# Layer 0 of a two-layer trunk: the turn of block 1, the order of the first products, and where weight rows 3 and 5 are split

## The chip, the cores and the metric

The kernel runs on one core of a Trainium2 chip. The metric is the device time of one execution in microseconds. The engines are TensorE (PE, with its weight loads PEld), VectorE (DVE), ScalarE (ACT), GpSimd (POOL) and the sync engine (SP), which only issues DMAs; ACT and POOL issue DMAs too.

## The reference

Two layers on x (512 tokens, 1024 channels, float32). Layer 0 mixes by causal pooling over windows of 2, 4, 8 and 16, layer 1 by differential attention; a dense SwiGLU of width 2816 follows in both.

```python
for i in range(DEPTH):                        # DEPTH = 2
    h = _multiscale_pool(x, ...) if i % 2 == 0 else _diff_attention(x, ...)
    x = _layernorm(ALPHA * x + h, ln_mix_g[i], ln_mix_b[i])
    x = _layernorm(ALPHA * x + _swiglu(x, w_gate[i], w_up[i], w_down[i]), ln_ffn_g[i], ln_ffn_b[i])

def _layernorm(x, g, b):
    return (x - mean) * lax.rsqrt(var + LN_EPS) * g + b

def _swiglu(x, w_gate, w_up, w_down):
    return (jax.nn.silu(x @ w_gate) * (x @ w_up)) @ w_down
```

The change lies where layer 0's mixer ends and its SwiGLU begins: the first normalization, the transposition of its result, and the first products with `w_gate` and `w_up`.

## The kernel before

**Split numbers.** A float32 matrix product is done as three products of rounded parts. Every operand is split into a high part (ScalarE casts it to the matmul's type, `split`, L123) and a low part (what is left, a subtraction, L124, on VectorE unless `low` names another engine). `mm3` (L147) issues high weights by high x, high weights by low x, low weights by high x.

**Rows of weights.** All weights lie in `in_wall` as rows of 128x1024. `fetch` (L107) loads a row with SP's queue into one of five `raw` buffers; a load waits until the buffer's last row is split, and all later loads of SP wait behind it. `ready(upto, low)` (L126) fetches five rows ahead and splits each row up to `upto`. Rows 0 and 1 are the pooling mixer's, rows 2 to 5 (w2 to w5) are the gate and up weights of the first two column blocks, 6 and 7 (g_4, g_5) of the third.

**The engines' order is the order of the code.** `manual_schedule` (L303) keeps each engine's instructions in program order, so an instruction that waits holds all behind it on its engine.

**The end of the mixer (L447 to L514).** The 512 tokens are four blocks of 128. For each block s: `mixed` multiplies the pooled values by the mixing weights into two banks of the accumulation memory, `summed` adds them to the residual `res` (L183) and takes statistics (L190), `spread_of` makes mean and variance (L196, L198) and GpSimd raises the variance to the power -1/2 (L199), `norm` applies both in place on VectorE (L208). `transposed` turns the block on TensorE into two banks of four 128x128 pieces (`pt`, L235). `turned` (block 0) applies gain and bias on ScalarE and splits the result into `xt`. Before `norm` of block 0, `split_pooled` casts the last pooled banks on ScalarE (L123) and subtracts on VectorE (L124).

**The turn of block 1 (`turned_apart`, L259).** For each bank, and in it for each piece, ScalarE applies gain and bias straight into the high part (L269), and VectorE the same in full precision into `y` (L272). When both banks are done, VectorE subtracts the high parts from `y` (L278). Both engines read the same bank, and one instruction waits for the other there.

**The first products (`ffn`, L821 to L845).** For the first three column blocks f the gate bank (`g`) and the up bank (`u`) are multiplied with the first 256 tokens (`lo` = 0, six products of 24 matmuls), then with the last 256 (`lo` = 256). The very first product is taken apart by banks of the turn (L649 to L658): for pieces 0 to 3 high by high, low by high, high by low, then the same for pieces 4 to 7. All others go piece by piece with `mm3`. `late` puts the turns of block 2 behind the product (1, 0) and of block 3 behind (1, 1). Behind the products come the gate (`gated`, L671), the residual's gain and bias with `gb` (L227, L228), sums of weights for the later Strassen stages (`load_terms`, L738, on GpSimd's queue), and, from the ninth column block on, Strassen products. All of these are the same in both kernels.

Of the kernel before, what the change touches and what calls it, by code (L numbers as in the profile page):

```python
# [23 lines left out]
KB = D // P  # L24
# [30 lines left out]
def trunk(ctx, tc, x, wall, pscale, lam_p, subln, table, lng, lnb, band, first, onehot, out):  # L55
    nc = tc.nc

    keep = ctx.enter_context(tc.tile_pool(name="keep", bufs=1))
# [7 lines left out]
    xt = keep.tile([P, 2, 2, KB, 256], F32R, name="xt")  # L66
# [40 lines left out]
    def fetch(upto):  # L107
        while fetched[0] < min(upto, total):
            c = fetched[0]
            raws[c] = keep.tile([P, 1024], F32, tag="raw", name=f"raw{c}", bufs=RAWS)  # L110
            nc.sync.dma_start(out=raws[c], in_=wall[rows_of_wall[c]])
            if c in added:
                nc.gpsimd.dma_start(out=raws[c], in_=wall[added[c]], accum_op=ALU.add)
            fetched[0] += 1

    def split(dst_h, dst_l, src, scale=1.0, low=None):
        if scale != 1.0:
            nc.scalar.mul(dst_h, src, scale)
            nc.vector.scalar_tensor_tensor(
                dst_l, src, scale, dst_h.bitcast(F32), op0=ALU.mult, op1=ALU.subtract  # L120
            )
        else:
            nc.scalar.copy(dst_h, src)  # L123
            (low or nc.vector).tensor_tensor(dst_l, src, dst_h.bitcast(F32), op=ALU.subtract)  # L124

    def ready(upto, low=None):  # L126
        while divided[0] < min(upto, total):
            c = divided[0]
            fetch(c + RAWS)
            h, l = weight_pair(f"w{c}")  # L130
            raw = raws.pop(c)
            if c in by_dma:
                nc.scalar.copy(h, raw)
                nc.scalar.mul(l, raw, -1.0)
                nc.gpsimd.dma_start(
                    out=l, in_=wall[rows_of_wall[c]].bitcast(F32R), accum_op=ALU.add
                )
# [92 lines left out]
    turns = {}  # L230
# [27 lines left out]

    def turned_apart(n, s):  # L259
        o = (s % 2) * P  # L260
        banks = turns.pop((n, s))
        ys = []
        for i, pt in enumerate(banks):
            y = keep.tile([P, 4, P], F32, tag="y", name=f"y{n}_{s}_{i}", bufs=2)
            for k in range(4):
                kk = 4 * i + k
                bias, scale = bT[:, n, kk : kk + 1], gT[:, n, kk : kk + 1]
                a = pt[:, k * P : (k + 1) * P]
                nc.scalar.activation(  # L269
                    xt[:, s // 2, 0, kk, o : o + P], a, AF.Identity, bias=bias, scale=scale  # L270
                )
                nc.vector.tensor_scalar(  # L272
                    y[:, k, :], a, scalar1=scale, scalar2=bias, op0=ALU.mult, op1=ALU.add
                )
            ys.append(y)
        for i, y in enumerate(ys):
            h, l = (xt[:, s // 2, j, 4 * i : 4 * i + 4, o : o + P] for j in range(2))
            nc.vector.tensor_tensor(l, y, h.bitcast(F32), op=ALU.subtract)  # L278

    def turn(n, s):  # L280
        transposed(n, s)
# [22 lines left out]
    with tc.tile_pool(name="pool", bufs=1) as pp:  # L304
# [166 lines left out]
        mixed(2, 0)  # L471
        summed(0, 1)
        spread_of(0, 0)
        ready(4, nc.gpsimd)
        split_pooled(1, 2, 3)
        norm(0, 0)
        tbh = pp.tile([33, HEADS], F32R, name="tbh")
# [18 lines left out]
        mixed(3, 1)  # L496
        turned(0, 0)
        turned_apart(0, 1)
        ready(5)
        stat(0, 2, 0)  # L500
        summed(2, 1)
        spread_of(0, 2)
        ready(6)
        norm(0, 2)
        summed(3, 0, 1)
        spread_of(0, 3)
# [19 lines left out]
    def ffn(layer, late):  # L526
        n = 2 * layer + 1
# [4 lines left out]
        with tc.tile_pool(name=f"ffn{layer}", bufs=1) as fp:  # L532
# [111 lines left out]
                if upto > len(chunks):  # L644
                    prepare(upto - len(chunks), upto - len(chunks))

            def product(acc, j, lo, hi, apart=False):
                h, l = halves[j]
                if apart:  # L649
                    for b in range(2):  # L650
                        for w, i in ((h, 0), (l, 0), (h, 1)):
                            for k in range(4 * b, 4 * b + 4):
                                nc.tensor.matmul(
                                    wide(acc, lo, hi), w[:, k * P : (k + 1) * P],
                                    x_at(k, lo, hi)[i], start=w is h and i == k == 0,
                                    stop=(i, k) == (1, KB - 1),
                                )
                    return  # L658
                for k in range(KB):
                    mm3(  # L660
                        wide(acc, lo, hi),
                        (h[:, k * P : (k + 1) * P], l[:, k * P : (k + 1) * P]),
                        x_at(k, lo, hi),
                        k == 0,
                        k == KB - 1,
                    )
# [12 lines left out]
            def sums_of_x():  # L679

                r0, r1, r2, r3 = spare(4), spare(15), spare(6), spare(17)

                def whole(t, a, b):
                    tt(t, quarter(a, 0, b).bitcast(F32), quarter(a, 1, b).bitcast(F32), op=ALU.add)

                def high(m, t):
                    nc.scalar.copy(xs[:, m, 0], t)  # L687

                def low(m, t):
                    tt(xs[:, m, 1], t, xs[:, m, 0].bitcast(F32), op=ALU.subtract)  # L690
# [24 lines left out]
                yield  # L715
# [106 lines left out]
            accs = [(bank(f"g{layer}_{f}"), bank(f"u{layer}_{f}")) for f in range(early)]  # L822
            load_terms(0)
            load_terms(1)
            sums = sums_of_x()
            for lo in (0, 256):
                for f in range(early):
                    for i in range(2):
                        product(
                            accs[f][i], 2 * f + i, lo, lo + 256, layer == f == i == lo == 0  # L830
                        )
                        if not lo and (f, i) in late:
                            late[f, i]()
# [95 lines left out]
            f = early  # L929
# [40 lines left out]
            banks = {}  # L970
            done = store if final else None
            for p in DOWN:
# [586 lines left out]
```

## Time and profile before

| | us |
|---|---|
| median of three runs | 953.36 (953.12 to 954.56) |
| the profiled execution | 953.28 |
| its span, first to last instruction | 951.5 |
| TensorE busy in the span | 931.8 (98%) |
| VectorE / ScalarE / GpSimd busy | 790.1 / 514.0 / 128.4 |

In the timelines a row is: start, duration, engine, line, operation, output<-inputs, shapes, count, and in brackets the idle time before it with what ended it. Starts count from the span's start. A matmul's row is longer than its pitch, since matmuls overlap; the difference of two starts is the time that one takes of TensorE.

### The profile page before, as it was taken

To read this page: it belongs to the slowest core of one execution; us is meant where nothing else is said; L and a number is where in the kernel's file an instruction comes from. 1 tells how busy PE (TensorE), PEld (TensorE's weight loads), DVE (VectorE), ACT (ScalarE), POOL (GpSimd) and SP (SyncE) were. 2 spreads that over 40 slices of the span, in tenths; PEclk is the share of its full clock that TensorE was granted. 3 is DMA by queue.
4 is the path that set the end of the run, shared out by engine and by line. 5 is a ranking of instruction groups with operands and counts; after the bars stand their busy time and mean duration, and the time that the engine had idled before them with its cause. 6 is when DMAs were issued, how large, how long until landed. Compare 5 with 4: busy or idle time off the path is not lost.

```text
span 951.5 us, 14946 instructions
## 1 busy us (share of the span) xinstructions
PE 931.8 (98%) x5712; PEld 830.7 (87%) x5712; DVE 790.1 (83%) x1165; ACT 514.0 (54%) x817; POOL 128.4 (13%) x153
## 2 busy tenths in 40 slices
PE   9799999999999999999999999999999999999996
PEld 8698899999988878887888878998899999988885
DVE  7859979999988579968887785779779999987778
ACT  6563245555554357766877862833344554564450
POOL 4121211110001201100211100211111110001101
PEclk9999999999999999999999999999999999999999
DMA  8477897885867996876576522396978886878942
GB/s 232 148 227 246 303 277 248 260 262 187 273 206 258 358 297 225 216 191 163 136 158 151 131 102 89 102 319 207 292 242 249 252 270 202 260 248 277 365 156 90
DMA packets 86038, 211.11 MB, mean 222 GB/s; under 512 B 15140, under 2 KB 26660, under 8 KB 85966
## 3 DMA queue, kind: packets, MB, share of 16 engines
q1 hardware_dynamic: 43420, 117.16, 37.2%
q0 software_dynamic: 18768, 58.20, 24.6%
q10 hardware_dynamic: 23778, 34.78, 10.2%
q8 instruction: 45, 0.74, 0.3%
q14 instruction: 27, 0.22, 0.1%
HBM read 173.40 MB, written 36.72 MB: 221 GB/s over the span
## 4 chain that ended last, share of the span: by engine, by line
PE 78%; DVE 9%; DMA 6%; ACT 3%; issue 2%; SPq 1%; POOL 0%; DVEq 0%; ACTq 0%; POOLq 0%
PE A L895 17%; PE C L895 8%; PE P L962 6%; PE B L895 4%; PE Q L962 3%; PE u L151 3%; PE u L150 3%; PE u L149 3%; PE g L151 3%; PE g L150 3%; PE g L149 3%; DMA r<-tsum 2%; PE va L1110 2%; PE s L1176 2%; DMA r<-in_wall 2%
## 5 line engine op out<-in xcount | busy, mean ns | idle before, releaser
L629 DVE TENSOR_TENSOR raw<-raw,raw 128x1024 f32<-128x1024 f32 x56 | 68.3, 1219 | 0.5
L123 ACT CAST xs<-hid 128x512 fp32r<-128x512 f32 (+1 forms) x60 | 34.7, 582 | 24.4 <-DVE hid L807 24.4
L124 DVE TENSOR_TENSOR xs<-hid,xs 128x512 fp32r<-128x512 f32 (+1 forms) x60 | 38.4, 642 | 7.8 <-ACT xs L123 7.8
L1192 ACT ACTIVATE p<-p,mn 128x128 f32<-128x128 f32 (+3 forms) x64 | 35.2, 552 | 12.4 <-DVE mn L1187 12.4
L249 ACT ACTIVATE y<-pt,bT,gT 128x128 f32<-128x128 f32 x72 | 27.1, 456 | 22.4 <-PE pt L235 22.3
L738 POOL DMA_DIRECT2D b<-in_wall x20 | 14.1, 708 | 171.4 <-DVE g_58l L635 66.4
L799 POOL DMA_DIRECT2D xs<-ssum x24 | 17.5, 727 | 140.2 <-PE Q L962 119.0
L671 DVE TENSOR_TENSOR hid<-sg,u 128x512 f32<-128x512 f32 x16 | 11.0, 686 | 27.7 <-PE u L151 16.9
L199 POOL TENSOR_TENSOR rs<-rs,mhalf 128x1 f32<-128x1 f32 x16 | 12.0, 751 | 155.4 <-DVE rs L198 111.8
L738 POOL DMA_DIRECT2D hid<-in_wall x24 | 18.8, 825 | 85.3 <-DMA tsum<-hid 39.5
L1187 DVE CUSTOM_DVE_ANT_0 p<-s,bias 128x128 f32<-128x128 f32 (+3 forms) x64 | 28.0, 485 | 0.7 <-PE s L1176 0.7
L775 ACT CAST v<-u 128x512 fp32r<-128x512 f32 x22 | 13.7, 622 | 27.2 <-DVE u L773 27.0
L190 DVE BATCH_NORM_STATS2 st<-res 128x6 f32<-128x512 f32 x32 | 22.2, 694 | 1.1
L921 ACT ACTIVATE sg<-sg 128x512 f32<-128x512 f32 x14 | 8.9, 634 | 26.0 <-DVE sg L914 26.0
L739 POOL DMA_DIRECT2D hid<-in_wall x12 | 14.8, 1234 | 50.1 <-DMA hid<-in_wall 50.1
L687 ACT CAST xs<-hid 128x1024 fp32r<-128x1024 f32 x8 | 8.4, 1052 | 23.9 <-DVE hid L704 11.6
L1176 PE MATMUL s<-heads 64*128 64x256 f32 (+2 forms) x168 | 20.0, 354 | 1.1 <-ACT heads L123 0.8
L124 DVE TENSOR_TENSOR xt<-y,xt 128x512 fp32r<-128x512 f32 x18 | 12.2, 689 | 8.9 <-ACT xt L123 8.9
L1176 PEld LDWEIGHTS s<-heads 64*128 64x128 f32 x168 | 14.1, 185 | 5.2 <-ACT heads L123 1.0
L910 DVE TENSOR_TENSOR hid<-C,hid 128x512 f32<-128x512 f32 x14 | 9.7, 691 | 10.8 <-PE C L895 9.3
L1206 DVE SCALAR_TENSOR_TENSOR p<-p,sm,p 128x128 f32<-128x128 f32 (+3 forms) x32 | 17.7, 552 | 1.1
L906 ACT COPY hid<-C 128x512 f32<-128x512 f32 x14 | 8.2, 588 | 18.3 <-PE C L895 18.3
(1194 smaller groups left out, 3672.4 us busy)
## 6 DMA issues: line engine op xcount, KB each, us to landing
raw<-in_wall SPq DMA_DIRECT2D x122, 512.0 KB, 4.9
r<-tsum SPq DMA_DIRECT2D x40, 512.0 KB, 4.4
hid<-in_wall POOLq DMA_DIRECT2D x36, 512.0 KB, 7.0
b<-in_wall POOLq DMA_DIRECT2D x30, 512.0 KB, 5.9
r<-in_wall SPq DMA_DIRECT2D x30, 512.0 KB, 5.1
tsum<-hid ACTq DMA_DIRECT2D x24, 512.0 KB, 5.5
ssum<-v ACTq DMA_DIRECT2D x22, 512.0 KB, 4.0
tsum<-b ACTq DMA_DIRECT2D x20, 512.0 KB, 5.0
```

The source lines that it names most:

```text
L123: nc.scalar.copy(dst_h, src)
L124: (low or nc.vector).tensor_tensor(dst_l, src, dst_h.bitcast(F32), op=ALU.subtract)
L149: nc.tensor.matmul(acc, ah, bh, start=start, stop=False)
L150: nc.tensor.matmul(acc, ah, bl, start=False, stop=False)
L151: nc.tensor.matmul(acc, al, bh, start=False, stop=stop)
L629: tt(t, raws[pair[0]], raws[pair[1]], op=ALU.add)
L738: nc.gpsimd.dma_start(out=t[:, j], in_=src[:, j])
L895: nc.tensor.matmul(o, w[:, c], x[:, kk, :], start=p in ("P1", "Q5", "P2") and f + kk + e == 0, stop=p in ("Q4", "Q3", "P2") and (f, kk, e) ...
L962: nc.tensor.matmul(accs[s], x[:, k, r], y[:, c], start=first and k == 0 and e == 0, stop=last and k == m - 1 and e == 2, skip_group_check= ...
L1176: nc.tensor.matmul(accs[c][:, :wide], a[r, qs], b[r, :wide], start=i == 0, stop=i == 2)
L1187: nc.vector.tensor_tensor_reduce(out=p, in0=accs[c][:, :w], in1=biases[h][:, w - 1 :: -1] if w < S else biases[h][:, ::-1], op0=ALU.add, o ...
L1192: nc.scalar.activation(p, p, AF.Exp, bias=mn[:, q, c : c + 1], scale=-1.0, accum_out=sm[:, q, c : c + 1],)
```

## The change

Three edits, all before the second half of the first products.

1. `turned_apart`: ScalarE makes the high part of bank 0 while VectorE makes the full values of bank 1. Then ScalarE copies bank 1's high part from VectorE's result, VectorE makes bank 0's full values, and subtracts bank 1 first, then bank 0.
2. The six products of the first 256 tokens are ordered by parts. The first (`by_half`): high by high and low by high for pieces 0 to 3, the same for pieces 4 to 7, then high by low for 4 to 7 and for 0 to 3. The five others (`by_part`): all high by high, all high by low, all low by high.
3. Row 3 is split behind the turn of block 1 instead of ahead of the last `split_pooled`, and its low part moves from GpSimd to VectorE; row 4 takes row 5's old place on VectorE, and row 5's low part moves to GpSimd.

```diff
@@ turned_apart @@
-        for i, pt in enumerate(banks):
-            y = keep.tile([P, 4, P], F32, tag="y", name=f"y{n}_{s}_{i}", bufs=2)
+        ys = [
+            keep.tile([P, 4, P], F32, tag="y", name=f"y{n}_{s}_{i}", bufs=2) for i in range(2)
+        ]
+        hs, ls = (
+            [xt[:, s // 2, j, 4 * i : 4 * i + 4, o : o + P] for i in range(2)] for j in range(2)
+        )
...
+        def in_full(i):
             for k in range(4):
-                nc.scalar.activation(
-                    xt[:, s // 2, 0, kk, o : o + P], a, AF.Identity, bias=bias, scale=scale
+                a, bias, scale = affine_of(i, k)
+                nc.vector.tensor_scalar(
+                    ys[i][:, k, :], a, scalar1=scale, scalar2=bias, op0=ALU.mult, op1=ALU.add
                 )
-                nc.vector.tensor_scalar(
-                    y[:, k, :], a, scalar1=scale, scalar2=bias, op0=ALU.mult, op1=ALU.add
-                )
-            ys.append(y)
-        for i, y in enumerate(ys):
-            h, l = (xt[:, s // 2, j, 4 * i : 4 * i + 4, o : o + P] for j in range(2))
-            nc.vector.tensor_tensor(l, y, h.bitcast(F32), op=ALU.subtract)
+
+        for k in range(4):
+            a, bias, scale = affine_of(0, k)
+            nc.scalar.activation(hs[0][:, k, :], a, AF.Identity, bias=bias, scale=scale)
+        in_full(1)
+        nc.scalar.copy(hs[1], ys[1])
+        in_full(0)
+        for i in (1, 0):
+            nc.vector.tensor_tensor(ls[i], ys[i], hs[i].bitcast(F32), op=ALU.subtract)
@@ the end of the mixer @@
         spread_of(0, 0)
-        ready(4, nc.gpsimd)
         split_pooled(1, 2, 3)
...
         turned_apart(0, 1)
-        ready(5)
+        ready(4)
         stat(0, 2, 0)
         summed(2, 1)
         spread_of(0, 2)
-        ready(6)
+        ready(5)
+        ready(6, nc.gpsimd)
         norm(0, 2)
@@ product @@
                 if apart:
-                    for b in range(2):
-                        for w, i in ((h, 0), (l, 0), (h, 1)):
-                            for k in range(4 * b, 4 * b + 4):
+                    for i, (w, e, ks) in enumerate(apart):
+                        for k in ks:
...
@@ ffn @@
+            ks = [range(4 * b, 4 * b + 4) for b in range(2)]
+            by_part = [(0, 0, range(KB)), (0, 1, range(KB)), (1, 0, range(KB))]
+            by_half = [(0, 0, ks[0]), (1, 0, ks[0]), (0, 0, ks[1]), (1, 0, ks[1])]
+            by_half += [(0, 1, ks[1]), (0, 1, ks[0])]
...
-                            accs[f][i], 2 * f + i, lo, lo + 256, layer == f == i == lo == 0
+                            accs[f][i], 2 * f + i, lo, lo + 256,
+                            None if layer or lo else by_part if f or i else by_half,
```

How the rows move on the engines. ScalarE, from the last pooled banks of the mixer (`pool_2`, `pool_3`) to the splits behind the turn of block 1 (`pt_0_*` and `y_0_*` belong to block 0, `pt_1_*` and `y_1_*` to block 1; w3h is row 3's high part). Before:

```order
L123 COPY w3h<-raw_325 128x1024
L123 COPY pooled<-pool_2_201 128x2x256
L123 COPY pooled<-pool_3_202 128x2x256
...
L269 ACTIVATE xt<-pt_1_0_436,bT,gT 128x128 x4
L269 ACTIVATE xt<-pt_1_1_437,bT,gT 128x128 x4
L123 COPY w4h<-raw_327 128x1024
L123 COPY w5h<-raw_329 128x1024
```

and with the change:

```order
L123 COPY pooled<-pool_2_201 128x2x256
L123 COPY pooled<-pool_3_202 128x2x256
...
L282 ACTIVATE xt<-pt_1_0_430,bT,gT 128x128 x4
L284 COPY xt<-y_1_1_467 128x4x128
L123 COPY w3h<-raw_325 128x1024
L123 COPY w4h<-raw_327 128x1024
L123 COPY w5h<-raw_329 128x1024
```

The cast of row 3 went from ahead of the pooled casts to behind the turn, and four of the turn's eight instructions became one copy.

GpSimd, from the power of block 0 (`rs_0`) to the first loads of weight terms into `hid`. Before:

```order
L199 TENSOR_TENSOR rs_0_362<-rs_0_362,mhalf 128x1
L124 TENSOR_TENSOR w3l<-raw_325,w3h 128x1024
L482 MEMSET line 8x128
L199 TENSOR_TENSOR rs_1_431<-rs_1_431,mhalf 128x1
L199 TENSOR_TENSOR rs_2_504<-rs_2_504,mhalf 128x1
L199 TENSOR_TENSOR rs_3_521<-rs_3_521,mhalf 128x1
L738 DMA hid_535<-in_wall 128x2x512 x2
```

and with the change:

```order
L199 TENSOR_TENSOR rs_0_362<-rs_0_362,mhalf 128x1
L490 MEMSET line 8x128
L199 TENSOR_TENSOR rs_1_425<-rs_1_425,mhalf 128x1
L199 TENSOR_TENSOR rs_2_495<-rs_2_495,mhalf 128x1
L124 TENSOR_TENSOR w5l<-raw_329,w5h 128x1024
L199 TENSOR_TENSOR rs_3_518<-rs_3_518,mhalf 128x1
L746 DMA hid_532<-in_wall 128x2x512 x2
```

The low part of row 3 left the place behind block 0's power, and that of row 5 came between the powers of blocks 2 and 3, ahead of the loads.

VectorE, from the turn of block 1 to the norm of block 2. Before:

```order
L272 TENSOR_SCALAR y_1_0_472<-pt_1_0_436,gT,bT 128x128 x4
L272 TENSOR_SCALAR y_1_1_481<-pt_1_1_437,gT,bT 128x128 x4
L278 TENSOR_TENSOR xt<-y_1_0_472,xt 128x4x128
L278 TENSOR_TENSOR xt<-y_1_1_481,xt 128x4x128
L124 TENSOR_TENSOR w4l<-raw_327,w4h 128x1024
...
L124 TENSOR_TENSOR w5l<-raw_329,w5h 128x1024
L208 TENSOR_SCALAR res<-res,mv_2_502,rs_2_504 128x1024
```

and with the change:

```order
L276 TENSOR_SCALAR y_1_1_467<-pt_1_1_431,gT,bT 128x128 x4
L276 TENSOR_SCALAR y_1_0_466<-pt_1_0_430,gT,bT 128x128 x4
L287 TENSOR_TENSOR xt<-y_1_1_467,xt 128x4x128
L287 TENSOR_TENSOR xt<-y_1_0_466,xt 128x4x128
L124 TENSOR_TENSOR w3l<-raw_325,w3h 128x1024
...
L124 TENSOR_TENSOR w4l<-raw_327,w4h 128x1024
L208 TENSOR_SCALAR res<-res,mv_2_493,rs_2_495 128x1024
```

The two banks changed places, and each split behind them is that of one row earlier.

More of the change, by code (lines that the diff above doesn't have):

```diff
@@ L260, in turned_apart, with affine_of @@
         o = (s % 2) * P
-        banks = turns.pop((n, s))
-        ys = []
-        for i, pt in enumerate(banks):
-            y = keep.tile([P, 4, P], F32, tag="y", name=f"y{n}_{s}_{i}", bufs=2)
-            for k in range(4):
[L266 to L269, printed above, removed]
-                    xt[:, s // 2, 0, kk, o : o + P], a, AF.Identity, bias=bias, scale=scale
-                )
-                nc.vector.tensor_scalar(
-                    y[:, k, :], a, scalar1=scale, scalar2=bias, op0=ALU.mult, op1=ALU.add
-                )
-            ys.append(y)
-        for i, y in enumerate(ys):
-            h, l = (xt[:, s // 2, j, 4 * i : 4 * i + 4, o : o + P] for j in range(2))
-            nc.vector.tensor_tensor(l, y, h.bitcast(F32), op=ALU.subtract)
+        pts = turns.pop((n, s))
+        ys = [
[4 more added lines that the diff above has]
+        )
+        def affine_of(i, k):
+            kk = 4 * i + k
+            return pts[i][:, k * P : (k + 1) * P], bT[:, n, kk : kk + 1], gT[:, n, kk : kk + 1]
+        def in_full(i):
+            for k in range(4):
+                a, bias, scale = affine_of(i, k)
+                nc.vector.tensor_scalar(
+                    ys[i][:, k, :], a, scalar1=scale, scalar2=bias, op0=ALU.mult, op1=ALU.add
+                )
+        for k in range(4):
[6 more added lines that the diff above has]
+            nc.vector.tensor_tensor(ls[i], ys[i], hs[i].bitcast(F32), op=ALU.subtract)
     def turn(n, s):
@@ L645, in ahead, with product @@
                     prepare(upto - len(chunks), upto - len(chunks))
-            def product(acc, j, lo, hi, apart=False):
+            def product(acc, j, lo, hi, apart=None):
                 h, l = halves[j]
                 if apart:
-                    for b in range(2):
-                        for w, i in ((h, 0), (l, 0), (h, 1)):
-                            for k in range(4 * b, 4 * b + 4):
[L653 to L657, printed above, removed]
+                    for i, (w, e, ks) in enumerate(apart):
+                        for k in ks:
+                            nc.tensor.matmul(
+                                wide(acc, lo, hi), (h, l)[w][:, k * P : (k + 1) * P],
+                                x_at(k, lo, hi)[e], start=i == 0 and k == ks[0],
+                                stop=i == len(apart) - 1 and k == ks[-1],
+                            )
                     return
```

## The prediction

> **What bounds the kernel now.** I read the page first, then the busy time by stretches, then the timeline of each engine up to 60 us, because the change touches nothing later. Two lines of the page:
>
> ```profile
> span 951.5 us, 14946 instructions
> PE 931.8 (98%) x5712; PEld 830.7 (87%) x5712; DVE 790.1 (83%) x1165; ACT 514.0 (54%) x817; POOL 128.4 (13%) x153
> ```
>
> TensorE sets the time. By stretches (busy TensorE, the granted clock, share and rate of the DMA engines):
>
> ```profile
> 39.00:42.30 3.30, 3.15 (x14) 0.50 0.07 11
> 43.00:300.00 257.00, 257.00 (x1820) 1.00 0.80 250
> ```
>
> From 43 us on TensorE has work without a break for 257 us, so whatever the start loses or saves goes to the end, as long as the weights keep up. The start does lose: in the first of these rows it runs at half the clock, and a wait of 3.35 us lies before it. TensorE's timeline at that place (start, duration, operation, in brackets the idle time and its releaser):
>
> ```profile
> 33.28 0.40 PE L653 MATMUL g<-xt,w2h 128*128 128x256 f32 x2
> 39.15 2.08 PE L653 MATMUL g<-xt,w2h 128*128 128x256 f32 x8 [3.35 <-DVE xt L278]
> 42.59 0.28 PE L149 MATMUL u<-xt,w3h 128*128 128x256 f32 x1
> 48.34 1.04 PE L235 MATMUL pt<-ident,res 128*128 128x128 f32 x8
> 49.13 0.36 PE L149 MATMUL u<-xt,w5h 128*128 128x256 f32 x1
> 52.08 1.04 PE L235 MATMUL pt<-ident,res 128*128 128x128 f32 x8
> 58.58 0.28 PE L151 MATMUL u<-xt,g_5l 128*128 128x256 f32 x1
> 58.70 0.28 PE L149 MATMUL g<-xt,w2h 128*128 128x256 f32 x1
> ```
>
> The first product runs from 33.28 to 42.59, 9.31 us. The last two rows show the pitch, 0.12 us, so its 24 matmuls are worth 2.88. The goal line is 58.70, where the second half of the columns begins: six products and two turns must lie before it, and I work out when the changed kernel gets there.
>
> **Term 1, weight row 3 leaves ScalarE's queue: 1.74 us gained.** The order before and after has this place ahead of the turn; its rows in the trace:
>
> ```profile
> 18.48 0.28 PE L411 MATMUL pool<-bh,xt 128*128 128x256 f32 x1
> 21.93 1.05 ACT L123 CAST w3h<-raw 128x1024 fp32r<-128x1024 f32 x1 [3.49 <-DMA raw<-in_wall]
> 22.89 1.07 ACT L123 CAST pooled<-pool 128x512 fp32r<-128x512 f32 x2
> 22.26 0.15 DVE L198 TENSOR_SCALAR rs<-mv 128x1 f32<-128x1 f32 x1
> 23.50 1.29 DVE L124 TENSOR_TENSOR pooled<-pool,pooled 128x512 fp32r<-128x512 f32 x2 [1.09 <-ACT pooled L123]
> 24.70 1.46 DVE L208 TENSOR_SCALAR res<-res,mv,rs 128x1024 f32<-128x1024 f32 x1
> 44.77 0.81 DVE L208 TENSOR_SCALAR res<-res,mv,rs 128x1024 f32<-128x1024 f32 x1 [0.44 <-POOL rs L199]
> 22.56 0.55 POOL L199 TENSOR_TENSOR rs<-rs,mhalf 128x1 f32<-128x1 f32 x1 [2.11 <-DVE rs L198]
> 23.09 2.41 POOL L124 TENSOR_TENSOR w3l<-raw,w3h 128x1024 fp32r<-128x1024 f32 x1
> ```
>
> ScalarE stood 3.49 us behind the transfer of row 3 while the pool banks behind it had been ready since about 18.8. Without it the two casts run at once, and VectorE's 1.09 us of idle time goes. The second piece is the 1.46 us of L208 at 24.70 against 0.81 at 44.77: it overlaps GpSimd's w3l, which ends at 25.50, and L208 ends 0.66 after that, at 26.16. Read so, it was held until GpSimd was done; with w3l gone from here 0.65 more go. Together 1.74: block 1's transposes move from 30.94 to 29.2, the first product from 33.28 to 31.54.
>
> **Term 2, the turn and the order of the product: 5.86 us gained.**
>
> ```profile
> 29.05 1.50 ACT L249 ACTIVATE y<-pt,bT,gT 128x128 f32<-128x128 f32 x4
> 30.58 0.62 ACT L123 CAST xt<-y 128x512 fp32r<-128x512 f32 x1
> 32.10 0.41 DVE L272 TENSOR_SCALAR y<-pt,gT,bT 128x128 f32<-128x128 f32 x1
> 32.55 0.46 ACT L269 ACTIVATE xt<-pt,bT,gT 128x128 fp32r<-128x128 f32 x1 [0.48 <-DVE y L272]
> 34.92 0.76 DVE L272 TENSOR_SCALAR y<-pt,gT,bT 128x128 f32<-128x128 f32 x2 [0.53 <-ACT xt L269]
> 38.41 1.28 DVE L278 TENSOR_TENSOR xt<-y,xt 128x512 fp32r<-128x512 f32 x2
> 39.61 1.22 DVE L124 TENSOR_TENSOR w4l<-raw,w4h 128x1024 fp32r<-128x1024 f32 x1
> ```
>
> Before, the two engines take turns on one bank, 0.94 us a piece (31.61 to 32.55). Apart, four pieces take ScalarE 1.5 us and VectorE 1.46 (pitch 0.35 from the pair of 0.76, plus 0.41). All new operations have such rows, so their cost is not open. After, in steps: ScalarE's bank 0 from 29.87 to 31.4; VectorE's bank 1 from 30.3 to 31.76; the copy 31.82 to 32.44; VectorE's bank 0 to 33.15; both subtractions (1.28) to 34.4. TensorE has its first eight matmuls ready at 31.54, the next eight follow to 33.46, then it waits to 33.9 and once more 0.1 for the low parts and is through at 35.0: 3.45 instead of 9.31. The cold stretch goes with the long wait. Row 3's cast now comes behind the copy (32.4 to 33.4), its low part on VectorE at 34.3 to 35.5; high weights go first, so w3l is needed 1.92 into its product, at 36.9, and covered by 1.4 us. w4l (below) ends at 39.0 and is needed at 39.8.
>
> **Term 3, what comes back: 2.8 us lost.** VectorE's sequence behind the turn is the same, moved by 39.61 - 34.3 = 5.3; TensorE is 7.6 early at 35.0. The other edit is here: row 5's low part goes to GpSimd, between two powers.
>
> ```profile
> 16.98 3.46 POOL L124 TENSOR_TENSOR w2l<-raw,w2h 128x1024 fp32r<-128x1024 f32 x1 [0.62 <-ACT w2h L123]
> 43.32 1.41 POOL L199 TENSOR_TENSOR rs<-rs,mhalf 128x1 f32<-128x1 f32 x1 [13.38 <-DVE rs L198]
> 43.10 1.23 DVE L124 TENSOR_TENSOR w5l<-raw,w5h 128x1024 fp32r<-128x1024 f32 x1
> 45.50 0.68 DVE L183 SCALAR_TENSOR_TENSOR res<-res,mix 128x512 f32<-128x512 f32 x1
> 49.38 0.81 DVE L208 TENSOR_SCALAR res<-res,mv,rs 128x1024 f32<-128x1024 f32 x1 [0.73 <-POOL rs L199]
> ```
>
> The power of block 2 took 1.41 us, to 44.73, 0.40 behind the end of VectorE's split; the same happens with w4l in w5l's place, so it ends at 39.4. Then GpSimd goes on with w5l at once, and VectorE's L208 of block 2 wants to start in the same moment. No row shows this race. The two ends: L208 runs freely (0.81, to 40.25), or it is held as at 24.70, until w5l's end plus 0.66. I take the second, since GpSimd needs no signal for its next instruction (w3l at 23.09 follows a power that ends at 23.11). At 2.41 for w5l, L208 ends at 42.5; at the 3.46 of w2l, at 43.5, which I keep as the bad end.
>
> TensorE has finished three products at 35.0 + 2 x 2.88 = 40.75 and waits to 42.6 for block 2's transposes (1.85). They take 0.8 (48.34 to 49.13), row 5's product ends at 46.3; w5l, ready at 41.8, is in time. VectorE needs 3.88 from L183 to the next L208 (45.50 to 49.38), so block 3 is normed at 47.1 and TensorE waits to 47.25 (0.95). With 0.86 for the transposes and 5.76 for two products it reaches the second half at 53.9 instead of 58.70. Block 3's ScalarE work, twice 1.50 + 0.62 from about 47.9, and the last subtraction (0.64) end near 52.8, so nothing waits there. Sum: 1.74 + 5.86 - 2.8 = **4.8 us**.
>
> The Trainium skill (SBUF — State Buffer, Who interferes with whom) speaks against the placing of w5l: a VectorE instruction in a two-port mode and a GpSimd one that reads SBUF shut each other out completely, and the one issued first wins. By that rule and the order taken here the sum is the same 4.8, with VectorE first it is that of the first rival; the 0.66 behind w3l's end agrees with it.
>
> **The queues.** SP's loads stay in order, but row 8's buffer is now freed at 35.5 instead of 25.50, and row 9's load and the two gb loads behind it wait for w5l (41.8; before, 40.86). GpSimd's first term loads come behind the later power, about 46.5 instead of 49.57. Who needs them:
>
> ```profile
> 41.23 0.43 SPq L177 DMA_DIRECT2D gb<-in_lng  x1
> 49.57 1.60 POOL L738 DMA_DIRECT2D hid<-in_wall  x2 [0.23 <-PE pt L235]
> 64.72 0.69 DVE L671 TENSOR_TENSOR hid<-sg,u 128x512 f32<-128x512 f32 x1 [6.60 <-PE u L151]
> ```
>
> VectorE first reads gb after the gate at 64.72, which becomes 59.9. That is 17 us behind its load, so I price these moves at nothing.
>
> **The rivals.** *VectorE gets in first* (20%): L208 runs its 0.81, w5l is held instead and still ends by 42.7. Block 2 costs no wait, block 3 about 0.6, the goal line moves to 51.6, a gain of 7.1: 946.2. For it speaks that the start order on the two engines differs by hundredths; against, w3l's row.
>
> *Weights don't keep up* (9%). In the first down projection the lead is small (first row: busy us of PE, PEld, DVE, ACT and POOL, the clock, the DMA engines' share and rate):
>
> ```profile
> 310.00:350.00 40.00, 39.54 (x175) 32.41 (x174) 24.09 (x27) 18.49 (x23) 8.23 (x10) 1.00 0.99 331
> L962 PE MATMUL P<-d_30l,xs x4: 388/394/397, 346.6 to 349.4; 128*128 128x512 f32 x4
> L124 DVE TENSOR_TENSOR d_30l<-r,d_30h x1: 1226/1226/1226, 344.1 to 344.1; 128x1024 fp32r<-128x1024 f32 x1
> ```
>
> The DMA engines are 99% busy and d_30l is ready 1.3 us ahead of its use (346.6 - 345.3). If that stretch stayed where it is, only 1.3 us would be left: 952.0. Against it: its loads are issued as TensorE and VectorE free their buffers, so it starts earlier too.
>
> *The clock halves again* (10%): TensorE waits 1.85 and 0.95 us. One stretch like 39.00 to 42.30 costs half of 3.3, so 950.1. Against it: the wait before 26.31 did nothing (1.00 below, TensorE busy 0.12 of 1.9 us).
>
> ```profile
> 24.40:26.30 1.90, 0.12 (x2) 0.02 (x1) 1.90 (x4) 0.17 (x1) 1.22 (x2) 1.00 0.95 390
> ```
>
> The Trainium skill (TensorE: Matmul & The Clock Gate, The HAM clock gate) lets the clock fall after a whole idle window of about 3.4 us, which neither wait fills; by it this rival would be worth nothing.
>
> *Slower* (6%): the same mechanism on all the new gaps (33.5, 40.75, 46.3), so that the clock stays at a half. It costs half of the time spent so; beyond 9.6 us of it the gain of 4.8 is gone, and through five products (14.4 us at full pitch) it costs 14.4: 962.9. The gaps would have to be taken for idleness though TensorE works between them.
>
> **How the numbers follow.** The sum stands against the profiled execution's 953.28 us (span 951.5 and 1.8 around it), 0.08 under the median of 953.36. Forecast (55%): 953.28 - 4.8 = 948.5, its own range 947.3 to 949.6 (w5l at 3.46 takes 1.0 more). With the first rival below and the clock's above, 945.8 to 950.8 holds over 8 in 10. About 0.2% (1.9 us) is what a measurement here can tell from no change: faster by more is forecast, first rival and clock, 85%; within it the weights' rival, 9%; slower 6%.
>
> **What would show it.** In the changed profile: pooled casts at 18.8 and L208 at 23.6 with 0.81 (term 1); the first product over in 3.5 us at clock 1.00 (term 2); L208 of block 2 at some 3 us beside w5l, and waits of 1.9 and 1 us before the two later turns (term 3); the second half at 53.9. Wrong would be a long wait in front of w5l, a granted clock under 1.00 after 40 us, or new waits behind 100 us.

## The result and the profile after

| | before | changed |
|---|---|---|
| median of 6 runs each, us | 953.63 (953.12 to 955.06) | 947.51 (947.25 to 947.70) |
| ratio, with its 95% interval | 1 | 0.9933 (0.992 to 0.9946) |
| span of the profiled execution, us | 951.5 | 945.5 |
| start of the second half of the columns (goal line), us | 58.70 | 53.26 |

The kernel became faster, by 6.1 us between the medians and 6.4 by the ratio (5.1 to 7.6 by its interval); 948.5 was forecast, with a range of its own from 947.3 to 949.6, so the time lies near the lower end of it. The page of the changed kernel:

```profile
span 945.5 us, 14942 instructions
PE 930.1 (98%) x5712; PEld 829.2 (88%) x5712; DVE 790.5 (84%) x1165; ACT 512.3 (54%) x814; POOL 128.3 (14%) x153
```

TensorE is still the engine that sets the time. Its busy time fell by 1.7 us (about half of the 3.3 us that had run at half the clock), and its idle time from 951.5 - 931.8 = 19.7 to 945.5 - 930.1 = 15.4 us, by 4.3. Together these are the 6.0 us of the span.

TensorE's timeline of the changed kernel from the first product on (start, duration, operation, in brackets the idle time and its releaser):

```profile
31.26 0.64 PE L661 MATMUL g<-xt,w2h 128*128 128x256 f32 x4
33.33 1.34 PE L661 MATMUL g<-xt,w2h 128*128 128x256 f32 x8
34.50 2.08 PE L661 MATMUL u<-xt,w3h 128*128 128x256 f32 x16
41.91 1.09 PE L235 MATMUL pt<-ident,res 128*128 128x128 f32 x8 [1.49 <-DVE res L208]
46.61 1.06 PE L235 MATMUL pt<-ident,res 128*128 128x128 f32 x8 [0.73 <-DVE res L208]
53.26 0.28 PE L149 MATMUL g<-xt,w2h 128*128 128x256 f32 x1
```

The first product takes 34.50 - 31.26 = 3.24 us instead of 9.31, where 24 matmuls at the pitch of 0.12 take 2.88. So 0.36 us are left of its waits for VectorE's low parts; the overlap of the matmul rows hides them from the brackets, but the eight matmuls with low parts start at 33.33 instead of 33.17 and take 1.17 us instead of 0.96. The longer waits now stand further down, in front of the transposes of blocks 2 and 3, and both name the norm (L208). By stretches (busy TensorE, granted clock, share and rate of the DMA engines):

```profile
31.00:36.00 5.00, 5.00 (x41) 1.00 0.00 2
36.00:43.00 7.00, 5.51 (x47) 1.00 0.31 91
43.00:50.00 7.00, 6.27 (x54) 1.00 0.98 373
50.00:300.00 250.00, 250.00 (x1739) 1.00 0.81 253
```

The clock is full throughout, in the two stretches that hold the waits too, and from 50 us TensorE works without a break, as it did from 43 before. ScalarE's timeline:

```profile
17.52 2.06 ACT L123 CAST pooled<-pool 128x512 fp32r<-128x512 f32 x4 [1.02 <-PE pool L420]
29.60 1.51 ACT L282 ACTIVATE xt<-pt,bT,gT 128x128 fp32r<-128x128 f32 x4 [0.23 <-PE pt L235]
31.43 0.62 ACT L284 CAST xt<-y 128x512 fp32r<-128x512 f32 x1 [0.33 <-DVE y L276]
```

The four pooled casts follow one another with no transfer in between, and the turn is one bank in 1.51 us and one copy. VectorE's:

```profile
22.09 0.15 DVE L198 TENSOR_SCALAR rs<-mv 128x1 f32<-128x1 f32 x1
23.36 0.81 DVE L208 TENSOR_SCALAR res<-res,mv,rs 128x1024 f32<-128x1024 f32 x1
30.03 2.64 DVE L276 TENSOR_SCALAR y<-pt,gT,bT 128x128 f32<-128x128 f32 x8
32.59 1.28 DVE L287 TENSOR_TENSOR xt<-y,xt 128x512 fp32r<-128x512 f32 x2
33.79 1.22 DVE L124 TENSOR_TENSOR w3l<-raw,w3h 128x1024 fp32r<-128x1024 f32 x1
37.29 1.23 DVE L124 TENSOR_TENSOR w4l<-raw,w4h 128x1024 fp32r<-128x1024 f32 x1
38.95 2.90 DVE L208 TENSOR_SCALAR res<-res,mv,rs 128x1024 f32<-128x1024 f32 x1 [0.44 <-POOL rs L199]
45.65 0.81 DVE L208 TENSOR_SCALAR res<-res,mv,rs 128x1024 f32<-128x1024 f32 x1 [0.73 <-POOL rs L199]
```

and GpSimd's:

```profile
37.50 1.41 POOL L199 TENSOR_TENSOR rs<-rs,mhalf 128x1 f32<-128x1 f32 x1 [9.57 <-DVE rs L198]
38.89 2.42 POOL L124 TENSOR_TENSOR w5l<-raw,w5h 128x1024 fp32r<-128x1024 f32 x1
```

L208 of block 0 is free now (0.81 instead of 1.46). L208 of block 2 has taken its place: it was 0.81 before and is 2.90 beside GpSimd's w5l, and it ends 0.54 us behind it (41.85 against 41.31). That is the new wait of this kernel, in the place where the forecast put it.

### The profile page after: what moved, and what is told of

Its sections match the earlier page's. It is cut to its first block, busy times and chain, and to the rows that moved or that the text cites. A ratio compares the mean times of both kernels' runs of the same rounds, so it can differ in the third digit from the quotient of the medians.

```text
span 945.5 us, 14942 instructions
## 1 busy us (share of the span) xinstructions
PE 930.1 (98%) x5712; PEld 829.2 (88%) x5712; DVE 790.5 (84%) x1165; ACT 512.3 (54%) x814; POOL 128.3 (14%) x153
## 4 chain that ended last, share of the span: by engine, by line
PE 82%; DVE 9%; ACT 3%; DMA 3%; issue 2%; POOL 0%; DVEq 0%; ACTq 0%; POOLq 0%
PE A L908 17%; PE P L975 9%; PE C L908 9%; PE B L908 4%; PE Q L975 3%; PE g L149 3%; PE u L149 3%; PE g L150 3%; PE u L150 3%; PE u L151 3%; PE g L151 3%; PE va L1123 2%; PE s L1189 2%; DMA r<-tsum 1%; PE k L149 1%
```

## The experiments

Executions differ by a microsecond or two in what the change doesn't touch (from the goal line to the end, the traces of the changed kernels have between 891.3 and 894.0 us), so medians alone can't tell half a microsecond. The sharper measure is a stretch inside one trace: from L198 of block 0 on VectorE (22.26 before, 22.09 changed) to the goal line on TensorE. Only work that the change touches lies in it, and any stretch that TensorE runs at half the clock there: 36.44 us before, 31.17 changed, so 5.27 gained. This table has it for all kernels, with two readings of VectorE from the same start: when L208 of block 2 starts, and when it ends.

| kernel | L208 of block 2 starts | ends | stretch to the goal line | median, us | ratio to before (95%) |
|---|---|---|---|---|---|
| before | 22.51 | 23.32 | 36.44 | | 1 |
| changed | 16.86 | 19.76 | 31.17 | 947.51 | 0.9933 (0.992 to 0.9946) |
| changed, again (e5) | 16.86 | 19.74 | 31.16 | 947.88 | 0.9933 (0.9919 to 0.9946) |
| rows as before (e1) | 18.60 | 19.41 | 30.83 | 947.51 | 0.9927 (0.9915 to 0.994) |
| rows only (e2) | 20.66 | 23.56 | 35.36 | 951.63 | 0.9981 (0.9972 to 0.999) |
| old product order (e3) | 16.87 | 19.77 | 31.18 | 947.67 | 0.993 (0.9918 to 0.9943) |
| gap of 0.2 us before row 5 (e4) | 16.87 | 19.92 | 31.33 | 947.50 | 0.9929 (0.9915 to 0.9942) |
| row 5 on VectorE (e6) | 17.48 | 18.29 | 29.70 | 946.09 | 0.9915 (0.9902 to 0.9929) |
| row 4 on GpSimd, row 5 on VectorE (e7) | 16.87 | 17.69 | 29.10 | 946.74 | 0.992 (0.9907 to 0.9934) |
| rows 4 and 5 on GpSimd (e8) | 16.01 | 19.06 | 30.49 | 947.04 | 0.9924 (0.9912 to 0.9937) |
| gap of 0.5 us before row 5 (e9) | 16.87 | 17.68 | 29.09 | 946.25 | 0.9928 (0.9906 to 0.995) |
| turn only (e10) | 18.60 | 19.41 | 31.73 | 949.14 | 0.9947 (0.9934 to 0.996) |
| e7 again (e11) | 16.86 | 17.67 | 29.10 | 945.86 | 0.9919 (0.9906 to 0.9932) |
| e6 again (e12) | 17.48 | 18.29 | 29.70 | 946.15 | 0.9922 (0.9909 to 0.9935) |

In all but three rows the goal line lies 11.41 to 11.43 us behind the end of that L208. There VectorE's chain of norms sets the pace, and what any edit is worth is what it does to this one instruction's end. The three others (before 13.12, rows only 11.80, turn only 12.32) are later than this chain: something on TensorE's side, the turn and the first product, is the later one.

In the edits, `ready(4)` splits weight row 3, `ready(5)` row 4 and `ready(6)` row 5, on VectorE unless `nc.gpsimd` is named.

### e1: the rows as before

```diff
         summed(0, 1)
         spread_of(0, 0)
+        ready(4, nc.gpsimd)
         split_pooled(1, 2, 3)
...
-        ready(4)
+        ready(5)
         stat(0, 2, 0)
         summed(2, 1)
         spread_of(0, 2)
-        ready(5)
-        ready(6, nc.gpsimd)
+        ready(6)
```

> Turn and product order as in the changed kernel, rows 3 to 5 split where they were before. Theory (VectorE's norms of blocks 2 and 3 set the pace behind the first product, and row 5 on GpSimd holds the first of them): the start is 1.7 us later again, but L208 of block 2 falls back from 2.90 to 0.81 us, TensorE waits about 0.5 us for block 3 only, and the time is that of the changed kernel, 947.1 +- 0.5. Rival (the edits add up and the row moves are a gain by themselves): 1.7 us more, 949.2.

Measured: 947.51, and 0.34 us less in the stretch than the change. VectorE's norm of block 2 and TensorE's last wait in this kernel:

```profile
40.60 0.81 DVE L208 TENSOR_SCALAR res<-res,mv,rs 128x1024 f32<-128x1024 f32 x1 [0.44 <-POOL rs L199]
```

```profile
46.17 1.06 PE L235 MATMUL pt<-ident,res 128*128 128x128 f32 x8 [0.35 <-DVE res L208]
```

L208 starts 1.74 us later than with the change (18.60 against 16.86 in the table) and is 2.09 shorter. So moving row 3 away from ScalarE's queue gains 1.74, as the first term says, and putting row 5 on GpSimd gives 2.09 back: on top of the turn and the order the row moves cost 0.34 us in the stretch, and the medians of the two kernels are the same.

### e2: the rows only

```diff
-        ready(4, nc.gpsimd)
         split_pooled(1, 2, 3)
...
-        ready(5)
+        ready(4)
         stat(0, 2, 0)
         summed(2, 1)
         spread_of(0, 2)
-        ready(6)
+        ready(5)
+        ready(6, nc.gpsimd)
```

This one is against the kernel before.

> The kernel before with the row moves alone. Theory: 1.7 us won at the start; L208 of block 2 takes about 3 us beside row 5's split on GpSimd, but TensorE is late by its first product and waits only some 0.5 us for block 3's norm; the second half starts 1.2 us earlier than before, time about 952.3. Rival (L208 is long for another reason than GpSimd's split, or the moves cost nothing later): 0.81 us there and 951.9.

Measured: 951.63, and 1.08 us gained in the stretch of the traced execution. (L198 started at 24.59 in this execution, against 22.00 to 23.16 in all others, because of a wait ahead of everything that was edited; its absolute starts are not compared.) L208 of block 2 on VectorE and row 5 on GpSimd:

```profile
45.25 2.90 DVE L208 TENSOR_SCALAR res<-res,mv,rs 128x1024 f32<-128x1024 f32 x1 [0.44 <-POOL rs L199]
```

```profile
45.19 2.42 POOL L124 TENSOR_TENSOR w5l<-raw,w5h 128x1024 fp32r<-128x1024 f32 x1
```

The held L208 is a product of the row move alone, whatever the turn does. With the old turn it costs nothing, since TensorE is late there anyway: block 2's transposes start at 49.57, 1.42 us behind its end, and among TensorE's waits up to 60 us none is for L208. The 0.5 us that were expected in front of block 3 didn't come.

Something else took 0.77 us here. Counted from L198 the first product starts 1.85 us earlier than before (9.17 against 11.02), and only 1.08 of that is left at the goal line. In this execution TensorE ran longer at half the clock (busy TensorE, clock, share and rate of the DMA engines):

```profile
36.30:37.70 1.40, 0.00 (x0) 1.00 0.02 6
37.80:39.60 1.80, 0.00 (x0) 0.50 0.00 0
39.60:44.50 4.90, 4.88 (x23) 0.50 0.36 111
```

Before, the clock was full again from 42.4 us on, after 3.2 us of work at half the clock; here it took 4.9, and half of the difference is about what is missing. This was the slowest of the eleven executions (954.57), and the ratio of all of them gives 1.8 us (1.0 to 2.7). So the rows alone are worth what they gain at the start, nearer to the rival's 951.9 than to the theory's 952.3.

### e3: the order of the first product as before

```diff
-                    for i, (w, e, ks) in enumerate(apart):
-                        for k in ks:
...
+                    for b in range(2):
+                        for w, i in ((h, 0), (l, 0), (h, 1)):
+                            for k in range(4 * b, 4 * b + 4):
...
-                            None if layer or lo else by_part if f or i else by_half,
+                            accs[f][i], 2 * f + i, lo, lo + 256, layer == f == i == lo == 0
```

> Turn and row moves as in the changed kernel, but the six products in the order of before (the first one by banks, the others piece by piece). Theory: the first product ends 1.4 us later (it needs bank 0's low part after eight matmuls, and that comes last), and TensorE then waits 1.4 us less for block 2's norm: the same time as the changed kernel, 947.5 +- 0.4. Rival (the order carries its share of the gain): 948.9.

Measured: 947.67, and a stretch of 31.18 against 31.17: nothing. The waits of TensorE up to 60 us (us in total, times, longest):

```profile
PE g L662 <- DVE xt L287: 1.5, 1, 1.5
PE pt L235 <- DVE res L208: 0.7, 1, 0.7
```

The changed kernel has 2.2 us in two waits, both for L208. Here the same 2.2 us stand in other places, because block 2's transposes can't begin before L208 ends at any rate. The first product itself takes 4.68 us here (31.77 to 36.45) instead of 3.24, so inside it the order is worth 1.44. An order that starts a product earlier is worth nothing in front of a wait that stays.

### e10: the turn only

The turn of the change in the kernel before; rows and order of the product as before (the diff is that of `turned_apart`, shown above).

> The kernel before with the new turn alone: product order and row places as before. Theory: the first product ends 1.4 us later than with the new order, TensorE then is behind VectorE's norms and waits for neither block, so 0.9 us are lost against the run with rows as before: 948.4, five of the six us of the whole change. Rival (the turn needs the new order to pay): more than 950.

Measured: 949.14, 4.71 us gained in the stretch, 0.90 less than e1, which differs from it by the order of the product alone. Here the order counts: L208 ends at 19.41 in both, but the goal line lies 12.32 behind it instead of 11.42, since the product starts late (row 3 is still in ScalarE's queue) and has the wait of 1.5 us inside. The stretch came out as expected; the 0.7 us by which the time missed lie outside it. Far behind it, this line of the waits is not in the changed kernel (e8 has its like, with 0.3):

```profile
PE P L971 <- ACT xs L123: 1.0, 1, 1.0
```

Whether that wait comes from the edit or from one execution, no second trace tells.

So the edits don't add up: rows alone 1.08 (about 1.8 without the longer stretch at half the clock), the turn alone 4.71, turn and order 5.61, all three 5.27.

### e4: a small gap ahead of row 5 on GpSimd

```diff
         ready(5)
+        nc.gpsimd.memset(pp.tile([8, P], F32, name="idle"), 0.0)
         ready(6, nc.gpsimd)
```

> The changed kernel with one small GpSimd instruction (a memset of 8x128, 0.2 us) between the power of block 2 and row 5's split. Theory (the one that issues first shuts out the other): VectorE's L208 now comes first and takes 0.81 us, row 5's split takes about 3.1 instead of 2.42, TensorE does not wait for block 2 and 0.5 us for block 3, 2.1 us won: 945.4. Rival (L208 is held by something else, or the two share): L208 stays at 2.9 us or both stretch, 947.5.

A miss. VectorE's L208, and GpSimd's memset and split, in this kernel:

```profile
39.37 3.05 DVE L208 TENSOR_SCALAR res<-res,mv,rs 128x1024 f32<-128x1024 f32 x1 [0.44 <-POOL rs L199]
```

```profile
39.29 0.20 POOL L512 MEMSET idle<- 8x128 f32 x1
39.45 2.41 POOL L124 TENSOR_TENSOR w5l<-raw,w5h 128x1024 fp32r<-128x1024 f32 x1
```

The memset moved w5l behind L208's start, by 0.08 us, and L208 was held all the same, 0.15 longer than without it. The theory that the recorded start decides is wrong. Two were left: the access that they share is needed only some way into L208, or GpSimd wins in any order.

### e9: a longer gap at the same place

```diff
         ready(5)
+        nc.gpsimd.tensor_tensor(pp.tile([P, 1], F32, name="idle"), eps_t, mhalf, op=ALU.pow)
         ready(6, nc.gpsimd)
```

> As the run with the small memset, but with a second power of 128x1 (0.55 us, on constants) between the power of block 2 and row 5's split. Theory (whoever holds the access keeps it; the 0.08 us of the memset were too short for L208 to get going): L208 now runs 0.81 us, row 5's split is held until it is over and takes about 2.7, TensorE waits for block 3 only: 2.1 us won against the changed kernel, 945.5. Rival (GpSimd's split goes ahead of a VectorE instruction that has started): L208 again ends 0.56 us behind the end of row 5's split, near 3.6 us long, and the time is 948.1.

```profile
38.87 0.81 DVE L208 TENSOR_SCALAR res<-res,mv,rs 128x1024 f32<-128x1024 f32 x1 [0.44 <-POOL rs L199]
```

```profile
38.80 0.91 POOL L512 TENSOR_TENSOR idle<-eps_t,mhalf 128x1 f32<-128x1 f32 x1
39.32 2.64 POOL L124 TENSOR_TENSOR w5l<-raw,w5h 128x1024 fp32r<-128x1024 f32 x1
```

With 0.45 us between the starts L208 runs freely, and it is w5l that stretches (2.64 instead of 2.42). The stretch is 29.09, 2.08 less than the change: the price of the held L208, measured by itself. So GpSimd doesn't win whatever the order. If GpSimd takes the shared access at its own recorded start, L208 needs it somewhere between 0.08 and 0.45 us after its own; the held ones of block 2 end 0.54 to 0.56 us behind GpSimd, which would put it at 0.81 - 0.55 = 0.26. That is argued, not shown: w5l's recorded start lies inside the row of the power ahead of it, which ends at 39.71, behind L208's end at 39.68. And that power started 0.07 us ahead of L208 without holding it.

The times show less than the stretch: 946.25, with one of six executions at 952.56 and an interval of the ratio that takes in that of the change. In the traced execution (946.82) some of the gain is lost again later: TensorE is busy 238.85 of the 240 us from 60 to 300, where the changed kernel has 240.00. Whether the earlier start causes these waits, one trace doesn't tell; e7, as early at the goal line by the stretch, has none there.

The Trainium skill (SBUF — State Buffer, Who interferes with whom) says that a VectorE instruction in a two-port mode and a GpSimd one that reads SBUF exclude each other, and that the one issued first wins. The exclusion agrees with these rows (2.90 and 3.05 against 0.81); the order of the recorded starts doesn't decide it, as e4 shows.

### e6 and e12: row 5 on VectorE

```diff
         ready(5)
-        ready(6, nc.gpsimd)
+        ready(6)
```

> The changed kernel with row 5's low part on VectorE, directly behind row 4's. Theory: VectorE pays 1.22 us more work, and the power on GpSimd is held by both splits (to about 40.0), but L208 of block 2 takes 0.81: TensorE waits 0.7 us for block 2 and 0.9 for block 3, 1.0 us won against the changed kernel, 946.5. Rival (GpSimd's split costs VectorE nothing, 1.22 us of work on VectorE's chain comes in): 1.2 us lost, 948.7.

> Row 5 on VectorE once more, on the same chip. Its trace had a wait of 0.7 us: 0.4 us over the run with rows 4 and 5 exchanged, 946.4, if the start is the same in both.

Measured: 946.09 and 946.15, 1.47 us less in the stretch, both times. VectorE's norm and GpSimd's power in e6:

```profile
39.52 0.81 DVE L208 TENSOR_SCALAR res<-res,mv,rs 128x1024 f32<-128x1024 f32 x1
```

```profile
37.46 1.41 POOL L199 TENSOR_TENSOR rs<-rs,mhalf 128x1 f32<-128x1 f32 x1 [9.57 <-DVE rs L198]
```

A split that takes VectorE another 1.14 us delays L208 by 0.62 only: the 0.44 us in which VectorE had stood still for GpSimd's power are filled, and no w5l holds L208. The power was expected to be held by both splits, to 40.0; it ended at 38.87, held by the first alone, and TensorE's one wait in brackets is for block 3 (0.74). That is about the difference between the 1.47 us won and the 1.0 expected. A fuller queue on the busy engine is cheaper here than help that blocks it.

### e7 and e11: rows 4 and 5 change places

```diff
         stat(0, 2, 0)
+        ready(5, nc.gpsimd)
         summed(2, 1)
         spread_of(0, 2)
-        ready(5)
-        ready(6, nc.gpsimd)
+        ready(6)
```

> The changed kernel with rows 4 and 5 exchanged: row 4's low part on GpSimd directly behind the first statistics of block 2, row 5's on VectorE. Theory: GpSimd's split (held by VectorE's split of row 3, then 2.4 us, to 37.4) is over before the power, L208 of block 2 takes 0.81 us from 38.95, TensorE waits only 0.5 us for block 3: 2.1 us won, 945.4. Rival (what is on GpSimd does not matter): 947.5.

> Rows 4 and 5 exchanged once more, beside the next. Its trace had TensorE waiting 0.4 us in front of the second half's turns where the changed kernel had 2.2: 1.5 to 2 us under the changed kernel's 947.7, 946.0.

Measured: 946.74 and 945.86; the stretch is 29.10 both times, 2.07 less than the change. GpSimd, VectorE's norm of block 2, and TensorE's one wait behind the first product in e7:

```profile
35.10 3.29 POOL L124 TENSOR_TENSOR w4l<-raw,w4h 128x1024 fp32r<-128x1024 f32 x1 [6.09 <-ACT w4h L123]
38.58 1.41 POOL L199 TENSOR_TENSOR rs<-rs,mhalf 128x1 f32<-128x1 f32 x1 [0.20 <-DVE rs L198]
```

```profile
40.03 0.82 DVE L208 TENSOR_SCALAR res<-res,mv,rs 128x1024 f32<-128x1024 f32 x1 [0.44 <-POOL rs L199]
```

```profile
45.61 1.06 PE L235 MATMUL pt<-ident,res 128*128 128x128 f32 x8 [0.36 <-DVE res L208]
```

GpSimd still splits a row, but ahead of the power instead of behind it, where nothing on VectorE waits for its end. It is w4l that gets stretched (3.29), and that costs nothing. This version is ahead of both kernels in the trace, twice by the same 2.07 us; the intervals of the ratios overlap with those of the change. On the one chip that ran both, though, all four executions of e7 (947.15 at most), and all four of e6, lie under all five of the change (947.24 at least). Between e6 and e7 the times show no difference, where the stretch has 0.60. No run removed the last 0.36.

### e8: both rows on GpSimd, with the small gap

```diff
         stat(0, 2, 0)
+        ready(5, nc.gpsimd)
...
-        ready(5)
+        nc.gpsimd.memset(pp.tile([8, P], F32, name="idle"), 0.0)
         ready(6, nc.gpsimd)
```

> Both low parts on GpSimd: row 4's ahead of the power of block 2, a memset of 8x128 and row 5's behind it. Theory: no two-input work of VectorE meets the power (0.55 instead of 1.41 us), L208 of block 2 runs at 38.0 with 0.81, row 5's split is held by it and ends near 41.2, in time for its product; TensorE waits for neither block: 2.6 us won, 944.9. Rival (GpSimd's 2.4 us splits come too late for their products or stretch VectorE): not under 946.

A miss, for e4's reason: L208 starts earlier than in any other kernel (16.01 in the table) and loses it again. The rows of VectorE and GpSimd:

```profile
38.76 3.05 DVE L208 TENSOR_SCALAR res<-res,mv,rs 128x1024 f32<-128x1024 f32 x1 [0.73 <-POOL rs L199]
```

```profile
38.84 2.42 POOL L124 TENSOR_TENSOR w5l<-raw,w5h 128x1024 fp32r<-128x1024 f32 x1
```

### e5: the change again

> The changed kernel itself, on the chip of the next three. Both theories: ratio to the kernel before 0.9935, L208 of block 2 at 2.90 us.

947.88 and a stretch of 31.16: what the stretch says of the change repeats to 0.01 us, while L198 itself started 0.57 later.

## Why the prediction was right, point by point

**Term 1 (row 3, 1.74).** Right. From L198 to the end of L208 of block 0 it was 26.16 - 22.26 = 3.90 us before and 24.17 - 22.09 = 2.08 after, so 1.82. Both pieces are there, ScalarE's casts without the transfer and L208 at 0.81. That this really comes from the place of row 3 is shown by e1, where L208 of block 2 falls back by 1.74, and by e2, where the first product starts 1.85 earlier with the rows alone.

**Term 2 (turn and order, 5.86).** Right in its mechanism, 6.07 in size. VectorE's eight pieces follow at a pitch of 0.32 us ((2.64 - 0.40) / 7, with 0.40 for the last), where 0.35 had been read from a pair; that brings the low parts forward, and the two small waits that were drawn inside the product came out at 0.36 us together instead of 0.57 (3.45 - 2.88). The prediction gave one sum for turn and order and didn't ask which of them carried it: inside the product the order is worth 1.44 (e3), but by the goal line it adds nothing with the rows moved, and 0.90 with the rows as before (e10 against e1).

**Term 3 (2.8 given back).** Right, and the choice in it too: L208 is held (2.90), not w5l. The reason given for the choice, that GpSimd goes on at once and so comes first, holds for the recorded starts here (38.89 against 38.95), but e4 shows that it doesn't decide: L208 is held as well when it starts 0.08 ahead. The stretch from the end of the first product to the goal line was 58.70 - 42.59 = 16.11 and is 53.26 - 34.50 = 18.76, so 2.65 were lost. The waits were forecast at 1.85 and 0.95 and are shown as 1.49 and 0.73. They are counted from the modelled end of the last matmul, 0.16 behind its pitch (0.28 against 0.12); with that they are 1.65 and 0.89. VectorE came to L208 0.5 us earlier than worked out: about 0.3 of it because the first product itself began earlier (31.26 instead of 31.54), the rest by the faster turn of term 2. Of the 2.65, 2.08 are the held L208 (e9); the rest is the wait for block 3's norm, which e9 keeps in part.

**The sum.** 1.82 + 6.07 - 2.65 = 5.24, where 4.8 was forecast; 0.03 between the norm and the first product and 0.17 that this execution started earlier make the goal line's 5.44. The mechanism was right and the size 0.4 short, half of it in term 2. From the goal line to the end it is 945.5 - 53.26 = 892.2 us, and 951.5 - 58.70 = 892.8 before; this is where the rest of the span's 6.0 comes from. The second execution of the changed kernel (span 945.5, goal line at 53.82) has 891.7 there, so such a difference is within what one kernel varies by.

**The queues** were priced at nothing. VectorE's first gate, behind which it reads gb, one of the loads that now wait for w5l, still waits for TensorE and for no load, 5.45 us earlier than before, and the reading of gb follows it without a wait:

```profile
59.27 0.69 DVE L679 TENSOR_TENSOR hid<-sg,u 128x512 f32<-128x512 f32 x1 [4.90 <-PE u L151]
```

**The rivals.** *VectorE gets in first* fell by the row at 38.95 (2.90); e9 brought its case about, and it is worth 2.08, where the prediction had 2.3 (7.1 - 4.8). *Weights don't keep up* fell: TensorE works through from 50 to 300 us, and in the down projection d_30l is first used 5.27 us earlier (341.30 instead of 346.57) without a wait in front of it. The lead in which the prediction saw the danger grew, from 1.3 to 1.9 us (d_30l is ready at 339.4). *The clock halves again* and *slower* fell by the clock of 1.00 from 31 to 50 us, with waits of 1.49 and 0.73 in it. In e3, e4, e5 and e8, with waits of up to 1.64 between 31 and 50 us, it stayed full too. The Trainium skill (TensorE: Matmul & The Clock Gate, The HAM clock gate) lets the clock fall after a whole idle window of about 3.4 us. These rows agree with it, and the row of before comes close, where 0.50 stands behind a wait of 3.35. The rows of e2 do not: there the clock was at 0.50 some 1.5 us into the wait (TensorE's last matmul ended at 36.28), with two short waits of 0.33 and 0.55 just ahead. Here the measurement decides: the rule alone was no ground to give this rival nothing, and the prediction kept 10% for it. What besides the length of one wait counts, no run here tells.

## What to carry to other kernels

When a long wait is removed, look for the chain that ends next and measure every edit against that one; here it was VectorE's norm of block 2. Row 3's place was worth 1.74 us because it moved that norm; the order of the product was worth 0.90 where TensorE was later than the norms, and nothing where it waited for them. Work that is moved to GpSimd to relieve VectorE belongs in a place where it is over before VectorE starts an instruction that it can hold, on the chain that ends last: row 5 behind the power cost 2.08 us, row 4 ahead of the power nothing. Edits that were made together are not worth the sum of what each is worth alone, so take one out of the whole as well as putting one in.

## What was not expected of the hardware

- Between L208 on VectorE and a split on GpSimd the recorded starts don't tell who is held. With a lead of 0.08 us L208 lost (3.05 and 3.05, in two kernels), with 0.45 it won (0.81). Where between the two the line is wasn't measured, and in the second case a small GpSimd instruction was still on record when L208 ended.
- A power on GpSimd, a 128x1 instruction, is stretched as well: 0.55 us alone, 0.91 beside L208 (the second one in e9), 1.41 when it starts 0.2 us into a split of VectorE's. Why the two lengths differ was not tried.
- The clock fell to a half after different waits: about 3.2 us after the end of TensorE's last matmul in the kernel before, about 1.5 in e2, though the wait was 3.35 us long in both; and it stayed there for 3.2 us of work in one, 4.9 in the other.
- Two engines on one PSUM bank in turns took 0.94 us for a pair of pieces, and on a bank each 0.38 (ScalarE, 1.51 for four) and 0.33 (VectorE, 2.64 for eight) a piece. The 0.94 are 0.41 of VectorE and 0.46 of ScalarE, one behind the other, and 0.07 between them.
